# Residual tokens parked in DRAM during the first expert product; their SBUF as gate sums and gated one-hots

## The chip, the cores and the metric

The kernel runs on one core of one Trainium2 chip. Its engines are TensorE (PE, matmuls; PEld are its weight loads), VectorE (DVE), ScalarE (ACT), GpSimd (POOL) and SyncE (SP, which issues nearly all DMAs). Every engine works through its own queue in order. On-chip memory is SBUF (128 partitions) and PSUM (eight banks, where PE writes). The metric is the device time of one execution in microseconds, the median of the runs.

## The reference

256 tokens of width 1024 go through two layers (retention, then differential attention, each followed by an expert block) and a second network (two gated feed-forwards around a mixer); all of it in float32. The part that the change touches is the expert block `peer_ffn`, which stands in both layers. Cut to what matters:

```python
q   = (xc @ w_q).reshape(tokens, 8, 2, 128)            # 8 heads, 2 halves
sc  = einsum('thpd,hpnd->thpn', q, subkeys)            # 128 scores for each half
s1, i1 = top_k(sc[:, :, 0], 16); s2, i2 = top_k(sc[:, :, 1], 16)
cand = s1[..., :, None] + s2[..., None, :]             # 256 candidates per head
top, pos = top_k(cand, 16)                             # 16 experts per head, of 128 x 128
gate = softmax(top)
act  = gelu(einsum('ted,td->te', u[idx], xc))
out  = einsum('te,ted->td', gate * act, v[idx])
x = layer_norm(alpha * x + out)
```

## The kernel before

The kernel gathers nothing. It computes the gelu of *all* 16384 experts for all tokens as a dense product, multiplies by a dense gate that is zero for experts not chosen, and makes a second dense product with `v`. Line numbers are those of the profile.

**Weights.** `stream` (L130) loads weights as tiles `raw` of 512 KB, four buffers, issued by SyncE; `split` (L121) makes from each a rounded copy `wh` on ACT (L125) and the residue `wl` on DVE (L126), three buffers each, so that three matmuls give nearly float32 precision. The splits are planned with a priority 300 places ahead of their position.

**The first expert product.** `peer` (L1165) holds H, 128 partitions x 128 x 256 float32, as its largest tile: partition and the second index `i2` name the expert, the last index the token. Before the loop, `x_transposed` makes the transposed tokens `xT` from the residual tokens `xs` (two tiles of 128 x 1024 float32; the layer norm's scale and shift are put in on the way, and `xs` itself gets them only later, in `affine`). A loop over 16 units computes the queries and the scores; `route_keys` and `route` pick the experts, in the part of H that the product hasn't reached yet. Then the loop over `i2` = 0 to 127 runs: `gemm_a` (L142) makes 24 matmuls (L147 to L149) into one of two PSUM banks `mm`, and ACT writes the gelu to `H[:, i2]` (L1245).

**The gates.** From `i2` = `K0` = 44 on the gates are built in the same loop, four tokens to a group, 64 groups. `onehots` (L1430) makes on DVE the raw one-hots `o12` (L1442, row and column of each of a token's 128 slots; named `o` in the trace) and the column's one-hots times the gate values, `og` (L1443). `gates` (L1446) has PE multiply them (L1453) into a PSUM tile `gat`; ACT copies one half (L1457) and DVE adds the other (L1460) to the dense gate of four tokens, `gate`, 128 x 512 float32. One step later `apply` multiplies the rows of H that are there by the gate (DVE, L1461) and writes the gate into the rows to come (ACT, L1463). For those later rows the product's gelu can't simply overwrite H: for the `nt` tokens whose gate is already in H, ACT writes the gelu to a tile `gelu` (L1250) and DVE multiplies it in (L1251); the rest goes straight to H (L1248). How many groups there are per step is set by

```python
e = (i2 + 2 - K0) * (T // 4) // (NKEYS - KEND - K0)
```

The pool `peer_u` has one buffer of each of its tiles (`xT`, `iota`, `og`, `gate`, `gelu`), the pool `peer_oh` two of `o12`.

**The second expert product.** The pools of the first product are closed; four PSUM banks `acc` replace those of the gates. For every `i2`, ACT and DVE split `H[:, i2]` into `gh` (L1285) and `gl` (L1286), and twelve matmuls (L1276) add to the four banks. At `i2` = 8 `affine` (L331) loads the norm's scale and shift by two broadcast DMAs (`ln_g`, `ln_b`, L293) and applies them to `xs` on DVE (L338, L339). `normalise` at the end is the next reader of `xs`.

**What sets the order.** The program is written in the order above, and a planner orders each engine's queue when it is built: it takes what is ready by its own estimate of times, earlier instructions first, and gives a tile from a pool only when a buffer of it is free. Waits between engines are derived from who reads and writes what, by regions of a tile.

Of the kernel before, what the change touches and what calls it, by code (L numbers as in the profile page):

```python
# [10 lines left out]
F32 = mybir.dt.float32  # L11
F32R = mybir.dt.float32r
F16 = mybir.dt.float16
# [7 lines left out]
T = 256  # L21
D = 1024
# [8 lines left out]
NKEYS = 128  # L31
# [16 lines left out]

AHEAD = 300
K0 = 44  # L50
KEND = 2
FOXN = 2
GSTEP = 6
PACE = 1
# [13 lines left out]
class Ker:  # L68
    def __init__(s, tc, A, ctx):
        s.tc = tc  # L70
        s.nc = nc = tc.nc
        s.A = A
        s.ctx = ctx
        s.cst = ctx.enter_context(tc.tile_pool(name="cst", bufs=1))
        s.rawp = ctx.enter_context(tc.tile_pool(name="rawp", bufs=4))
        s.hlp = ctx.enter_context(tc.tile_pool(name="hlp", bufs=3))
        s.ident = s.cst.tile([128, 128], F32, name="ident")
        s.ahead = AHEAD
        s.hold = []
        s.psn = 0  # L80
        s.ssq = s.cst.tile([128, 2, 2], F32, name="ssq")
        small = s.cst.tile([128, NSMALL], F32, name="small")
        s.last_tr = [None, None]
        s.zeros = s.cst.tile([128, 256], BF16, name="zeros")
        nc.gpsimd.memset(s.zeros, 0.0)
        s.small = small
        at = 0
        for n, w in SMALL:
            setattr(s, n, small[:, at:at + w])
            at += w  # L90
        s.events = []
# [563 lines left out]
    def mixer(s, xs, units_r, units_f, units_g, units_ra, units_fb, units_o):  # L655
        nc, A = s.nc, s.A
        with ExitStack() as cx:
# [41 lines left out]
            with ExitStack() as c1:  # L699
# [61 lines left out]
                for i in range(8):  # L761
                    next(fox, None)
                    with s.after(s.mark):
                        if i + FOXN < 8:
                            e = i + FOXN
                            unit_r(1 + e // 4, e % 4, w["rv"[e // 4]])
                    if i == BDAT:
                        next(prep)
                        s.rwkv_blocks(0, 0, w, bd0)
                    if i >= 8 - NGATE:  # L770
                        with s.after(s.mark):
                            next(gates, None)
# [4 lines left out]
            with ExitStack() as c1:  # L777
# [9 lines left out]
                while nxt < 8 or live:  # L787
                    if nxt < 8 and len(live) < LIVE:
                        live.append((nxt, todo[nxt]))
                        nxt += 1  # L790
                    for it in list(live):
                        step += 1
                        if step >= GS0 and (step - GS0) % GSTEP == 0:
                            assert s.mark
                            with s.tc.issue_after(s.mark), s.tc.high_priority(offset=LOW):
                                next(gates, None)
                        for _ in range(2):
                            if next(it[1], None) is None:
                                if it in live:
                                    live.remove(it)  # L800
                                    if it[0] < 8 and it[0] % 2:
                                        live.append((8 + it[0] // 2, tails[it[0] // 2]))
                                break
# [361 lines left out]
    def peer(s, l, xs, units_q, units_u, units_v, ln):  # L1165
        nc, A = s.nc, s.A
        with ExitStack() as cx:
# [3 lines left out]
            H = hp.tile([128, NKEYS, T], F32, name="H")  # L1171
            cu = ExitStack()
            p = s.pool("peer_u", 1, cu)
            s.iota = p.tile([128, 128], F16, name="iota")
            nc.sync.dma_start(s.iota, A["iota"])
            with ExitStack() as ct:
                xT = s.x_transposed(p, xs, "xT", s.ln_cols(ln), s.pool("peer_t", 2, ct))
            po = s.pool("peer_oh", 2, cu)

            off = [K0 * T]  # L1180

            def carve(shape, dt=F32):
                n = int(np.prod(shape[1:]))
                words = n if dt != F16 else (n + 1) // 2
                ap = H.rearrange("p a b -> p (a b)")[:, off[0]:off[0] + words]
                off[0] += words
                assert off[0] <= NKEYS * T
                if dt != F32:
                    ap = ap.bitcast(dt)
                if len(shape) == 2:  # L1190
                    return ap
                names = "abcde"[:len(shape) - 1]
                return ap.rearrange("p (%s) -> p %s" % (" ".join(names), " ".join(names)),
                                    **{k: v for k, v in zip(names, shape[1:])})
# [7 lines left out]
            def restart():  # L1202
# [7 lines left out]
            rt = {"s16": carve([128, 2, 16, TOPK]), "i16": carve([128, 2, 16, TOPK], U32),  # L1210
                  "tmp": [carve([128, NKEYS]) for _ in range(4)]}
            def scores(c):
                ps = s.aux()[:, :T].rearrange("p (a b) -> p a b", a=2)
                for tt in range(2):
                    nc.tensor.matmul(ps[:, tt], qT[:, c, tt * 128:tt * 128 + 128], sk[:, c], start=True, stop=True)
                nc.scalar.activation(sc[:, :, c], ps, AF.Copy)
# [17 lines left out]
            g = 0  # L1234
            pend = []
            for i2 in range(NKEYS):
                ps = s.mm()[:, :T]
                s.gemm_a(next(units_u), xT, ps)
                if i2 < 2:
                    if i2 == 0:  # L1240
                        scores(15)
                    s.route_keys(rt, sc, 14 + i2)
                nt = 4 * g
                if nt == 0:
                    nc.scalar.activation(H[:, i2], ps, AF.Gelu_apprx_tanh)  # L1245
                else:
                    if nt < T:
                        nc.scalar.activation(H[:, i2, nt:], ps[:, nt:], AF.Gelu_apprx_tanh)  # L1248
                    ge = p.tile([128, T], F32, name="gelu")
                    nc.scalar.activation(ge[:, :nt], ps[:, :nt], AF.Gelu_apprx_tanh)  # L1250
                    nc.vector.tensor_tensor(H[:, i2, :nt], H[:, i2, :nt], ge[:, :nt], op=ALU.mult)  # L1251
                if 2 <= i2 < K0:
                    for _ in range(ROUTE_STEPS):
                        next(route, None)
                    if i2 == K0 - 1:
                        for _ in route:
                            pass
                elif i2 >= K0:
                    for f in pend:
                        f(i2 + 1)  # L1260
                        g += 1
                    e = (i2 + 2 - K0) * (T // 4) // (NKEYS - KEND - K0)
                    pend = [s.gates(H, p, s.onehots(p, po, rt, j), j) for j in range(g, min(e, T // 4))]
            assert g * 4 == T
            cu.close()
            cg.close()
            s.banks(cx, "acc", 4)
            p2 = s.pool("peer_v2", 3, cx)
            p = s.pool("peer_v", 1, cx)
# [11 lines left out]
            for i2 in range(NKEYS):  # L1281
# [3 lines left out]
                a = nc.scalar.activation(wh, H[:, i2], AF.Copy).ins  # L1285
# [11 lines left out]
            a, b, c = last  # L1297
# [129 lines left out]
                                         [128, 128, 2, 2]), AF.Copy)  # L1427
            yield

    def onehots(s, p, p2, rt, g):  # L1430

        nc = s.nc
        sh = [128, 8, 64, 2]
        t4 = slice(4 * g, 4 * g + 4)
        tok = lambda t: t[:, t4].rearrange("p t a e -> p (t a) e")[:, :, None, :].to_broadcast(sh)
        v = lambda t: t.rearrange("p t a (k e) -> p (t a) k e", e=2)
        o = p2.tile([128, 4, 2, 128], F16, name="o12")
        og = p.tile([128, 4, 2, 128], F16, name="og")  # L1440
        io = s.iota.rearrange("p (k e) -> p k e", e=2)[:, None].to_broadcast(sh)
        nc.vector.tensor_tensor(v(o), io, tok(rt["I"]), op=ALU.is_equal)  # L1442
        nc.vector.tensor_tensor(v(og), o[:, :, 1:2].to_broadcast([128, 4, 2, 128]), tok(rt["G"]), op=ALU.mult)  # L1443
        return o[:, :, 0], og

    def gates(s, H, p, oh2, g):  # L1446


        nc = s.nc
        o1, og = oh2  # L1450
        ps = s.pgat.tile([128, 4, 2, 128], F32, name="gat")
        for t in range(4):
            nc.tensor.matmul(ps[:, t], o1[:, t], og[:, t], start=True, stop=True)  # L1453
        pv = ps.rearrange("p t a i -> p a i t")
        ts = slice(4 * g, 4 * g + 4)
        gt = p.tile([128, NKEYS, 4], F32, name="gate")
        nc.scalar.activation(gt, pv[:, 1], AF.Copy, scale=1.0 / GSCALE)  # L1457

        def apply(k):
            nc.vector.scalar_tensor_tensor(gt, pv[:, 0], 1.0 / GSCALE, gt, op0=ALU.mult, op1=ALU.add)  # L1460
            nc.vector.tensor_tensor(H[:, :k, ts], H[:, :k, ts], gt[:, :k], op=ALU.mult)  # L1461
            if k < NKEYS:
                nc.scalar.activation(H[:, k:, ts], gt[:, k:], AF.Copy)  # L1463

        return apply
# [190 lines left out]
```

## Time and profile before

| | |
|---|---|
| median of 3 runs | 2747.91 us (2747.08 to 2750.75) |
| the profiled execution's own time | 2750.62 us |
| its span | 2748.8 us |
| PE busy | 2674.3 us, 97% |
| DVE busy | 2004.6 us, 73% |
| ACT busy | 1472.8 us, 54% |
| POOL busy | 7.8 us |
| DMA | 450.49 MB, mean 164 GB/s |

Matmuls are pipelined: a matmul of 256 columns is listed with 0.28 us, but the next begins 0.12 us later. Idle time of an engine is put down to the instruction before which it stood, with the instruction that released it. Where a wait is listed for PE, the matmul before it counts as busy until its modelled end.

### The profile page before, as it was taken

What the parts mean: (1) busy time and instruction counts of PE and PEld (TensorE: products, weight loads), DVE (VectorE), ACT (ScalarE), POOL (GpSimd) and SP (SyncE); (2) the same over time, 40 slices, a digit from 0 to 9 for tenths busy, and PEclk for the clock granted to TensorE, in tenths of its full rate; (3) what the DMA queues carried; (4) which work ended last, traced back from release to release, by engine and by line L of the source; (5) the groups of instructions that cost most, each with busy time, mean ns of one, the idle gap of its engine ahead of it and who ended that gap; (6) DMA issues with size and microseconds to landing.
All of it is one profiled execution on the core that took longest, in us unless ns stands there. A gap on an engine that the chain in (4) does not pass through costs nothing. (4 is left out here: it accounts for less than half of the span.)

```text
span 2748.8 us, 44032 instructions
## 1 busy us (share of the span) xinstructions
PE 2674.3 (97%) x16550; PEld 2360.8 (86%) x16550; DVE 2004.6 (73%) x3688; ACT 1472.8 (54%) x2575; POOL 7.8 (0%) x24
## 2 busy tenths in 40 slices
PE   9999999999999999999999999999999999999999
PEld 7789999988788888789999888888878887887887
DVE  7559968899666668789788997666687567665674
ACT  4445556555555555555466555555555465543554
POOL 0000000000000000000000000000000000000000
PEclk9999999999999999999999999999999999999999
DMA  6454554444566654345554445666655553222554
GB/s 209 154 183 164 185 178 161 154 146 154 191 193 194 195 193 162 99 161 181 178 165 152 152 154 181 194 192 193 196 173 187 190 168 109 70 70 67 171 187 151
DMA packets 124420, 450.49 MB, mean 164 GB/s; under 512 B 14336, under 2 KB 15120, under 8 KB 123952
## 3 DMA queue, kind: packets, MB, share of 16 engines
q1 hardware_dynamic: 124064, 447.62, 50.1%
q8 instruction: 130, 2.13, 0.3%
q14 instruction: 82, 0.67, 0.1%
q10 hardware_dynamic: 144, 0.07, 0.0%
HBM read 446.57 MB, written 1.05 MB: 163 GB/s over the span
## 5 line engine op out<-in xcount | busy, mean ns | idle before, releaser
L126 DVE TENSOR_TENSOR wl<-raw,wh 128x1024 fp32r<-128x1024 f32 x830 | 1014.6, 1223 | 430.6 <-ACT wh L125 429.3
L125 ACT ACTIVATE wh<-raw 128x1024 fp32r<-128x1024 f32 x830 | 879.3, 1060 | 671.3 <-PE mm L148 332.4
L147 PE MATMUL mm<-xT,wh 128*128 128x256 f32 x2384 | 685.9, 288 | 29.8 <-ACT gelu L1250 26.6
L149 PE MATMUL mm<-xT,wl 128*128 128x256 f32 x2384 | 677.3, 284 | 1.8 <-DVE wl L126 1.8
L148 PE MATMUL mm<-xT,wh 128*128 128x256 f32 x2384 | 677.7, 284 | 0.0
L147 PEld LDWEIGHTS mm<-xT,wh 128*128 128x128 f32 x2384 | 457.3, 192 | 39.7 <-ACT gelu L1250 33.4
L149 PEld LDWEIGHTS mm<-xT,wl 128*128 128x128 f32 x2384 | 457.7, 192 | 2.9 <-DVE wl L126 2.4
L148 PEld LDWEIGHTS mm<-xT,wh 128*128 128x128 f32 x2384 | 458.2, 192 | 0.8 <-DVE xT L261 0.3
L1276 PE MATMUL acc<-wl,gh 128*128 128x512 f32 x1024 | 318.4, 390 | 0.3
L1276 PE MATMUL acc<-wh,gl 128*128 128x512 f32 x1024 | 317.3, 390 | 0.0
L1276 PE MATMUL acc<-wh,gh 128*128 128x512 f32 x1024 | 279.2, 391 | 6.8 <-ACT gh L1285 6.8
L1285 ACT ACTIVATE gh<-H 128x256 fp32r<-128x256 f32 x256 | 106.5, 418 | 300.9 <-PE acc L1276 300.9
L1276 PEld LDWEIGHTS acc<-wh,gh 128*128 128x128 f32 x1024 | 192.8, 188 | 47.3 <-ACT gh L1285 7.2
L1276 PEld LDWEIGHTS acc<-wl,gh 128*128 128x128 f32 x1024 | 193.0, 188 | 41.4 <-DVE wl L126 1.1
L1276 PEld LDWEIGHTS acc<-wh,gl 128*128 128x128 f32 x1024 | 192.8, 188 | 40.0
L1286 DVE TENSOR_TENSOR gl<-H,gh 128x256 fp32r<-128x256 f32 x256 | 108.4, 425 | 121.9 <-PE acc L1276 121.9
L159 PE MATMUL mm<-xT,wh 128*128 128x512 f32 x406 | 145.9, 397 | 0.8 <-ACT wh L125 0.6
L160 PE MATMUL mm<-xT,wl 128*128 128x256 f32 x406 | 114.1, 281 | 0.8 <-DVE wl L126 0.8
L1443 DVE TENSOR_TENSOR og<-o,slotG 128x1024 f16<-128x1024 f16 x128 | 88.1, 688 | 29.8 <-PE gat L1453 28.8
L159 PE MATMUL aux<-xT,wh 128*128 128x512 f32 x294 | 105.0, 394 | 0.0
L182 PE MATMUL acc<-wl,xT 128*128 128x512 f32 x256 | 103.2, 404 | 0.0
L183 PE MATMUL acc<-wh,xT 128*128 128x512 f32 x256 | 101.8, 400 | 0.0
(539 smaller groups left out, 3859.7 us busy)
## 6 DMA issues: line engine op xcount, KB each, us to landing
raw<-peer_u SPq DMA_DIRECT2D x256, 512.0 KB, 3.8
raw<-peer_v SPq DMA_DIRECT2D x256, 512.0 KB, 4.6
raw<-ffn_w SPq DMA_DIRECT2D x132, 512.0 KB, 4.4
raw<-peer_q SPq DMA_DIRECT2D x32, 512.0 KB, 3.9
raw<-ret_qk SPq DMA_DIRECT2D x16, 512.0 KB, 3.4
raw<-ret_v SPq DMA_DIRECT2D x16, 512.0 KB, 4.0
raw<-ret_g SPq DMA_DIRECT2D x16, 512.0 KB, 3.8
raw<-ret_o SPq DMA_DIRECT2D x16, 512.0 KB, 3.2
```

The source lines that it names most:

```text
L125: a = nc.scalar.activation(h, ap, AF.Copy)
L126: d = nc.vector.tensor_tensor(l, ap, h.bitcast(F32), op=ALU.subtract)
L147: nc.tensor.matmul(out, w[0][:, c], x[0][:, d], start=start and d == 0, stop=False)
L148: nc.tensor.matmul(out, w[0][:, c], x[1][:, d], start=False, stop=False)
L149: nc.tensor.matmul(out, w[1][:, c], x[0][:, d], start=False, stop=stop and d == ND - 1)
L159: nc.tensor.matmul(ps, w[0][:, c], x, start=d == 0, stop=False)
L160: nc.tensor.matmul(ps[:, :T], w[1][:, c], both[:, d, 0], start=False, stop=False)
L182: nc.tensor.matmul(outs[tt], x[0][:, d, t], w[1][:, c], start=False, stop=False)
L183: mm = nc.tensor.matmul(outs[tt], x[1][:, d, t], w[0][:, c], start=False, stop=stop and j == 1)
L1276: mm = nc.tensor.matmul(accs[cb][tt], a[:, t], b[:, cb * 512:cb * 512 + 512], start=i2 == 0 and wi == 0, stop=i2 == NKEYS - 1 and wi == 2)
L1285: a = nc.scalar.activation(wh, H[:, i2], AF.Copy).ins
L1286: d = nc.vector.tensor_tensor(wl, H[:, i2], wh.bitcast(F32), op=ALU.subtract).ins
```

## The change

Three things. A DRAM tile `spill` is made for the two residual tiles. After `xT` is there, both tiles of `xs` are copied to it by GpSimd's DMA, and the memory of `xs` is used for other things until the first product is over: `xs[0]` as two gate sums (`gsum`, in place of the tile `gate`) and `xs[1]` as two tiles of gated one-hots (`gated`, in place of `og`), taken by the group's number modulo two. After the loop the residual tokens are copied back. Second, `gelu` moves to the pool `peer_oh`, which gets three buffers: three of `o12` and three of `gelu`. Third, `KEND` goes from 2 to 3, so that the last group of gates is built one step of `i2` earlier.

```diff
--- before.py
+++ after.py
@@ -48,7 +48,7 @@
 
 AHEAD = 300
 K0 = 44
-KEND = 2
+KEND = 3
 FOXN = 2
 GSTEP = 6
 PACE = 1
@@ -81,6 +81,8 @@
         s.ssq = s.cst.tile([128, 2, 2], F32, name="ssq")
         small = s.cst.tile([128, NSMALL], F32, name="small")
         s.last_tr = [None, None]
+        dram = ctx.enter_context(tc.tile_pool(name="dram", bufs=1, space=bass.MemoryType.DRAM))
+        s.spill = dram.tile([2, 128, D], F32, name="spill")
         s.zeros = s.cst.tile([128, 256], BF16, name="zeros")
         nc.gpsimd.memset(s.zeros, 0.0)
         s.small = small
@@ -1175,7 +1177,12 @@
             nc.sync.dma_start(s.iota, A["iota"])
             with ExitStack() as ct:
                 xT = s.x_transposed(p, xs, "xT", s.ln_cols(ln), s.pool("peer_t", 2, ct))
-            po = s.pool("peer_oh", 2, cu)
+            po = s.pool("peer_oh", 3, cu)
+
+            for tt in range(2):
+                nc.gpsimd.dma_start(s.spill[tt], xs[tt])
+            s.gsum = xs[0].rearrange("p (b i t) -> p b i t", b=2, t=4)
+            s.gated = xs[1].bitcast(F16).rearrange("p (b t a k) -> p b t a k", b=2, t=4, a=2)
 
             off = [K0 * T]
 
@@ -1246,7 +1253,7 @@
                 else:
                     if nt < T:
                         nc.scalar.activation(H[:, i2, nt:], ps[:, nt:], AF.Gelu_apprx_tanh)
-                    ge = p.tile([128, T], F32, name="gelu")
+                    ge = po.tile([128, T], F32, name="gelu")
                     nc.scalar.activation(ge[:, :nt], ps[:, :nt], AF.Gelu_apprx_tanh)
                     nc.vector.tensor_tensor(H[:, i2, :nt], H[:, i2, :nt], ge[:, :nt], op=ALU.mult)
                 if 2 <= i2 < K0:
@@ -1260,10 +1267,12 @@
                         f(i2 + 1)
                         g += 1
                     e = (i2 + 2 - K0) * (T // 4) // (NKEYS - KEND - K0)
-                    pend = [s.gates(H, p, s.onehots(p, po, rt, j), j) for j in range(g, min(e, T // 4))]
+                    pend = [s.gates(H, s.onehots(po, rt, j), j) for j in range(g, min(e, T // 4))]
             assert g * 4 == T
             cu.close()
             cg.close()
+            for tt in range(2):
+                nc.gpsimd.dma_start(xs[tt], s.spill[tt])
             s.banks(cx, "acc", 4)
             p2 = s.pool("peer_v2", 3, cx)
             p = s.pool("peer_v", 1, cx)
@@ -1427,7 +1436,7 @@
                                          [128, 128, 2, 2]), AF.Copy)
             yield
 
-    def onehots(s, p, p2, rt, g):
+    def onehots(s, p, rt, g):
 
 
 
@@ -1436,14 +1445,14 @@
         t4 = slice(4 * g, 4 * g + 4)
         tok = lambda t: t[:, t4].rearrange("p t a e -> p (t a) e")[:, :, None, :].to_broadcast(sh)
         v = lambda t: t.rearrange("p t a (k e) -> p (t a) k e", e=2)
-        o = p2.tile([128, 4, 2, 128], F16, name="o12")
-        og = p.tile([128, 4, 2, 128], F16, name="og")
+        o = p.tile([128, 4, 2, 128], F16, name="o12")
+        og = s.gated[:, g % 2]
         io = s.iota.rearrange("p (k e) -> p k e", e=2)[:, None].to_broadcast(sh)
         nc.vector.tensor_tensor(v(o), io, tok(rt["I"]), op=ALU.is_equal)
         nc.vector.tensor_tensor(v(og), o[:, :, 1:2].to_broadcast([128, 4, 2, 128]), tok(rt["G"]), op=ALU.mult)
         return o[:, :, 0], og
 
-    def gates(s, H, p, oh2, g):
+    def gates(s, H, oh2, g):
 
 
         nc = s.nc
@@ -1453,7 +1462,7 @@
             nc.tensor.matmul(ps[:, t], o1[:, t], og[:, t], start=True, stop=True)
         pv = ps.rearrange("p t a i -> p a i t")
         ts = slice(4 * g, 4 * g + 4)
-        gt = p.tile([128, NKEYS, 4], F32, name="gate")
+        gt = s.gsum[:, g % 2]
         nc.scalar.activation(gt, pv[:, 1], AF.Copy, scale=1.0 / GSCALE)
 
         def apply(k):
```

## Rows read from the trace of the kernel before

**Rows 1.** The page's engine table: busy us, share of the span, instructions.

```profile
PE 2674.3 (97%) x16550; PEld 2360.8 (86%) x16550; DVE 2004.6 (73%) x3688; ACT 1472.8 (54%) x2575; POOL 7.8 (0%) x24
```

**Rows 2.** Stretch, length; busy us of PE, PEld, DVE, ACT, POOL; granted clock; DMA share; GB/s.

```profile
400.00:500.00 100.00, 97.28 (x812) 94.92 (x812) 84.26 (x139) 61.81 (x131) 0.00 (x0) 1.00 0.50 163
500.00:600.00 100.00, 94.42 (x787) 91.64 (x786) 90.30 (x147) 57.51 (x131) 0.00 (x0) 1.00 0.46 150
600.00:687.00 87.00, 80.40 (x664) 77.13 (x663) 80.67 (x124) 48.63 (x113) 0.00 (x0) 1.00 0.46 151
687.00:691.00 4.00, 0.72 (x7) 0.51 (x5) 3.12 (x6) 1.77 (x5) 0.00 (x0) 1.00 0.43 137
692.00:695.00 3.00, 3.00 (x9) 2.32 (x8) 0.23 (x1) 0.42 (x1) 0.00 (x0) 0.52 0.95 355
...
1500.00:1600.00 100.00, 92.73 (x767) 89.37 (x768) 91.72 (x147) 56.84 (x131) 0.00 (x0) 1.00 0.46 149
```

**Rows 3.** Waits of PE, whole span: who for whom, us, times, longest.

```profile
PE mm L147 <- ACT gelu L1250: 26.6, 24, 1.4
PE acc L1276 <- ACT gh L1285: 6.8, 2, 3.4
...
PE gat L1453 <- DVE og L1443: 3.1, 4, 0.8
```

**Rows 4.** Timeline of waits at L147: start, us, engine, line, tiles, idle before.

```profile
436.85 0.61 PE L1453 MATMUL gat<-og,o 128*128 128x256 f16 x4
438.37 0.38 PE L147 MATMUL mm<-xT,wh 128*128 128x256 f32 x1 [0.91 <-ACT gelu L1250]
...
541.86 0.28 DVE L1251 TENSOR_TENSOR H<-H,gelu 128x124 f32<-128x124 f32 x1
...
542.00 0.61 PE L1453 MATMUL gat<-og,o 128*128 128x256 f16 x4
542.08 1.06 ACT L125 ACTIVATE wh<-raw 128x1024 fp32r<-128x1024 f32 x1 [1.42 <-PE mm L148]
...
543.20 0.59 ACT L1457 ACTIVATE gate<-gat 128x512 f32<-128x512 f32 x1
...
543.68 0.28 ACT L1250 ACTIVATE gelu<-mm 128x128 f32<-128x128 f32 x1
...
544.01 0.39 PE L147 MATMUL mm<-xT,wh 128*128 128x256 f32 x1 [1.40 <-ACT gelu L1250]
...
550.31 0.61 PE L1453 MATMUL gat<-og,o 128*128 128x256 f16 x4
...
550.67 0.36 PE L147 MATMUL mm<-xT,wh 128*128 128x256 f32 x1
```

**Rows 5.** Waits of DVE before L1443, and L1443 in the list of instructions.

```profile
DVE og L1443 <- PE gat L1453: 28.8, 62, 0.9
...
L1443 DVE TENSOR_TENSOR og<-o,slotG 128x1024 f16<-128x1024 f16 x128 | 88.1, 688 | 29.8 <-PE gat L1453 28.8
```

**Rows 6.** Timeline of the change from the first product to the second.

```profile
687.71 0.68 DVE L1461 TENSOR_TENSOR H<-H,gate 128x504 f32<-128x504 f32 x1
...
690.38 0.38 ACT L1250 ACTIVATE gelu<-mm 128x256 f32<-128x256 f32 x1 [1.59 <-DVE H L1251]
690.66 1.02 ACT L1285 ACTIVATE gh<-H 128x256 fp32r<-128x256 f32 x3
...
691.13 0.74 PE L1276 MATMUL acc<-wh,gh 128*128 128x512 f32 x2 [3.41 <-ACT gh L1285]
```

**Rows 7.** Where `xs` is first written, and the nearest DMA, with us to landing.

```profile
709.80 2.35 DVE L338 TENSOR_TENSOR x<-x,ln_g 128x1024 f32<-128x1024 f32 x2
...
ln_b<-ln SPq DMA_DIRECT2D x4, 512.0 KB, 5.8
```

## The prediction

> **What bounds the kernel now.** I read the page's engine table first: TensorE (PE) is busy for 97% of the span and VectorE (DVE) is the next engine [rows 1]. So only time in which PE stands still can be won, and the question is how much of it belongs to the stage that the change touches. That stage is the second part of each first expert product: the loop over `i2` in `peer`, from `K0` on, in which the gates are built beside the product. It lies at about 410 to 687 us in the first layer and 1380 to 1660 us in the second.
>
> The busy table by stretches [rows 2] shows what changes inside it. PE idles 2.7 us in 400 to 500, 5.6 us in 500 to 600 and 6.6 us in 600 to 687, while DVE's busy time goes from 84.3 of 100 to 90.3 of 100 to 80.7 of 87: the gated part of H grows, and with it DVE's multiplications. The second layer has the same shape (PE 92.7 of 100 in 1500 to 1600). Two more things stand there: from 687 to 691 PE is busy for 0.72 us of 4, and from 692 to 695 its granted clock is 0.52 of full speed, which is the lower of its two levels (1.2 against 2.4 GHz); before that fall it had stood still.
>
> PE's table of waits [rows 3] names the causes: 26.6 us in 24 waits for L1250, the partial gelu, 12 of them in each layer; 6.8 us in 2 waits for L1285 where the second product starts; 3.1 us in 4 waits for L1443, the gated one-hots. The timeline of one wait [rows 4] shows the chain. The row of L1251 at 541.86 reads the only `gelu` tile until 542.14. Before that ScalarE (ACT) may not write the next gelu; at 542.08 it takes up the next weight copy instead, then a gate copy, and writes that gelu from 543.68 on. The gelu is what empties a PSUM bank of the product, there are two, so PE's next step begins at 544.01. From the gate product at 542.00 that is 2.01 us. In the undisturbed case in the same rows (550.31 to 550.67) it is 0.36 us. So the wait costs 1.65 us where the table shows 1.40; the short kind (436.85 to 438.37) costs 1.16 where it shows 0.91. Each wait costs 0.25 us more than it shows.
>
> **The change part by part.**
>
> *Three gelu tiles in place of one.* The 24 waits cost 26.6 + 24 x 0.25 = 32.6 us. With three tiles a gelu waits for a multiplication three steps back, and the link at 542.14 is gone.
>
> *Two gate sums and two gated one-hots, in the memory of `xs`, and three raw one-hots.* The four waits for L1443 cost 3.1 + 4 x 0.25 = 4.1 us. DVE itself idles 28.8 us before L1443, waiting for PE to have read the only `og` [rows 5]; a second buffer lets DVE do one pair of one-hots more ahead (a pair is two operations of about 0.69 us, so 1.4 us). The gate sum's wait on ACT is off PE's path except where a gelu stands behind it, which is in the 24 already.
>
> What is late next is DVE. By stretches, one layer loses 2.7 + 3 x 0.25 = 3.5 us, 5.6 + 4 x 0.25 = 6.6 us and 6.6 + 7 x 0.25 = 8.4 us, 18.5 us in all. In the first two DVE idles 15.7 and 9.7 us, more than PE has to win. In the last it idles 6.3 us: it can't do the same work in 8.4 us less. With the pair done ahead, 7.7 us at the most; no engine is filled to the end, so I take 6.5. From the first two I take off 1 us, for a wait or two that find another cause. That is 3.5 + 6.6 - 1 + 6.5 = 15.6 us per layer.
>
> *The last gates one step earlier (`KEND` 3).* The number of groups is the same (64 per layer) and so is the work, spread over 81 steps in place of 82. What moves is the end: now the last multiplication of H by a gate (L1461) begins at 687.71, when the product's matmuls are through, and lasts 0.68 us; after that ACT still waits 1.59 us for the gelu tile (gelu at 690.38), copies gh at 690.66, and PE starts at 691.13 [rows 6]. With the change the last gate is a step earlier and no gelu waits for its tile. What is left of the 3.41 us is a weight copy that may already be running on ACT (1.06 us), a gelu (690.38 to 690.66) and gh up to PE's start (0.47 us), 1.6 us if they overlap a little with the product's end. I take a gain of 1.8 us; the ends are 0, if gh stays behind something else, and 3.4.
>
> *The clock.* The fall in 692 to 695 costs at least 0.48 x 3 = 1.4 us per layer. Waits of up to 1.40 us leave the clock at 1.00 in the stretches before; the wait of 3.41 us is followed by a fall. With 1.6 us I count half: 0.7 us.
>
> *The spill and the restore.* Two DMAs of 512 KB out and two back per layer, issued by GpSimd. No GpSimd DMA is in this trace; the nearest row is that of `ln_b`, 512 KB in 5.8 us on SyncE's queue. The spill has no reader or writer behind it until the first gated one-hot, over 100 us later. The restore may start when the last gate sum is read and must be in before L338, which writes `xs` at 709.80 [rows 7]: 709.80 - 687.71 - 0.68 = 21.4 us for work of 2 x 5.8 = 11.6 us if the two don't overlap at all. Hidden, then: price 0 to 11.6 us per layer, and no gain, since transfers are only added. It shares the DMA engines with the second product's weights and with `ln_g` and `ln_b`, which load at the same place; the share is already 0.95 in 692 to 695. I put 0.5 us per layer for a late weight tile. If the cover is gone, DVE stands at L338 and the weight residues behind it (L126) are late for PE. The new wait before the first write into `xs` (for the spill) costs nothing for the same 100 us.
>
> *The order.* The instruction order is a planner's, made when the program is built, so every queue of the stage will be ordered anew. What that does elsewhere I take as 0, between -2 and +2 us, which is what the single small waits of PE are worth (the 1.59 us wait in rows 6 is the size of one).
>
> Sum per layer: 15.6 + 1.8 + 0.7 - 0.5 = 17.6 us, twice 35 us. The profiled execution took 2750.62 us (span 2748.8), so it would take 2715.6; the median of the runs is 2747.91, 2.7 us lower, so I predict 2713 us.
>
> **The rivals.**
>
> *Everything comes back.* All of 18.5 + 3.4 + 1.4 = 23.3 us per layer, 46.6 in all: 2701 us. For it: the three causes are all lack of a buffer. Against it: DVE's 6.3 us in the last stretch. Chance 0.15.
>
> *DVE fills up earlier.* Its work that now waits moves in front of PE's needs, and the last stretch gives nothing. Then the first two stretches give about half, 5 us, and the transition 1.8: 2 x 6.8 = 14 us, 2734 us. For it: DVE 93% busy in 600 to 687. Against: L126 is planned ahead of everything else on DVE. Chance 0.16.
>
> *It doesn't do what it says.* The gelu stays behind a gate copy on ACT because that waits for DVE anyway (in rows 4 the gate copy at 543.20 stands directly ahead of the late gelu), and the waits only get another name: 2748 us, within 4. Chance 0.06.
>
> *Slower: the restore is late.* The place is L338 on DVE at 709.80. DVE now spends 2.35 us there on the first two operations and PE doesn't stop, so some 3 us of lateness are free; from there each us costs PE one, in both layers. It decides the sign when it eats 17.6 us, so when the restore lands 20.6 us after 709.80, 42 us after the last gate, 3.6 times as long as the 11.6 us above. At 25 us late it is 2 x (22 - 17.6) = 9 us slower: 2757 us. For it: a GpSimd DMA isn't priced in this trace and DVE is nearly full as it starts. Against: the margin. Chance 0.05.
> The Trainium skill ("SBUF — State Buffer", section "SBUF: two separate sides") says that GpSimd can't write the descriptors of its DMAs while DVE runs an operation in a mode that takes both of its ports, which would speak for this rival. Its section "Who interferes with whom" adds that `tensor_tensor` has no such mode, and DVE's rows between 687 and 709 us here are all tensor-tensor forms; no run so far shows a GpSimd DMA beside them.
>
> **How the numbers follow.** The forecast has 0.58, with a range of its own from 2704 to 2724 (gains of 44 to 24 us: the last stretch and the transition at their ends). The 80% range goes from 2699 to 2736: it takes in the full return and DVE filling up, and leaves out no change and the late restore. About 0.2% of this time, 5.5 us, is what a measurement can tell from no change. Faster by more: 0.15 + 0.58 + 0.16, less 0.01 for the tails, 0.88. Within: 0.06. Slower: 0.05 and 0.01 for an order that turned out badly, 0.06.
>
> **What would show it.** PE's waits for L1250 fall from 24 to a few, those for L1443 vanish; DVE's wait before L1443 shrinks and DVE is busy for over 95% towards the end of the stage; the wait for L1285 is about 1.6 us; the stretch after it shows the clock at 1.00 in at least one layer; the restore has landed well before L338 and L338 doesn't wait. Wrong would be: as many waits before L147 with another releaser (L126 or a gate copy), a stage as long as before, DVE standing at L338, or a gain outside these two stages.

## The result, and the profile after

The changed kernel takes 2720.55 us (median of 4 runs, 2718.90 to 2721.53) against 2747.49 us before (4 runs): 26.9 us less, a ratio of 0.990 with a 95% interval from 0.9883 to 0.9917. A second set of runs of the same kernel gave 2720.81 us and 0.989 (0.9871 to 0.9910). The forecast was 35 us less, 2713 us, in a range from 2699 to 2736. The profiled execution took 2719.57 us (span 2717.8), 31.0 us less than the profiled one of before.

Lines have moved by two to nine: L147 is now L149, L1250 L1257, L1251 L1258, L1276 L1285, L1285 L1294, and L338 is L340; the gate sum and the gated one-hots show as `x`, since they lie in the memory of `xs` (L1443 is L1452, L1457 L1466, L1461 L1470, L1463 L1472).

PE's waits, whole span, against [rows 3]:

```profile
PE mm L149 <- ACT gelu L1257: 8.4, 6, 1.4
PE acc L1285 <- ACT gh L1294: 3.4, 2, 1.7
```

Of 24 waits for the gelu 6 are left, all of the long kind, three in each layer; the waits for the one-hots are gone; the wait at the second product's start has halved (3.41 us in [rows 6], 1.71 now). Where the six stand is in the busy table of the first layer, against [rows 2] (columns as there; the product ends at about 673 us now):

```profile
400.00:500.00 100.00, 100.00 (x842) 98.30 (x841) 88.02 (x149) 61.87 (x138) 0.00 (x0) 1.00 0.52 167
500.00:600.00 100.00, 100.00 (x842) 98.33 (x842) 94.45 (x154) 59.96 (x140) 0.00 (x0) 1.00 0.51 165
600.00:666.00 66.00, 61.78 (x515) 59.80 (x514) 62.46 (x97) 36.13 (x86) 0.00 (x0) 1.00 0.47 155
...
672.00:676.00 4.00, 2.29 (x15) 1.93 (x14) 3.19 (x6) 2.35 (x6) 0.54 (x1) 1.00 0.92 267
676.00:680.00 4.00, 4.00 (x19) 3.13 (x18) 2.72 (x7) 1.52 (x3) 0.00 (x0) 1.00 0.93 304
```

PE doesn't stop at all between 400 and 600 us. Every wait for the gelu that is left in this layer lies after 600 us, where DVE is busy for 62.46 of 66 us. Behind the start of the second product (676 to 680) the clock is at 1.00, where it had fallen to 0.52 before.

The copies: the timeline of the first layer's end (start, us, engine, line, what) and the issues with KB and us to landing.

```profile
670.70 0.54 POOL L1275 DMA_DIRECT2D x<-spill  x1 [457.12 <-DVE H L1258]
...
674.92 0.54 POOL L1275 DMA_DIRECT2D x<-spill  x1 [3.67 <-ACT gh L1294]
674.98 0.73 PE L1285 MATMUL acc<-wh,gh 128*128 128x512 f32 x2 [1.71 <-ACT gh L1294]
...
692.15 2.35 DVE L340 TENSOR_TENSOR x<-x,ln_g 128x1024 f32<-128x1024 f32 x2
```

```profile
spill<-x POOLq DMA_DIRECT2D x4, 512.0 KB, 3.5
...
x<-spill POOLq DMA_DIRECT2D x4, 512.0 KB, 6.5
```

The second restore is issued at 674.92; the longest landing of any of these copies is 8.8 us, so `xs` is whole by about 684, 8 us ahead of L340 (L338 in [rows 7]), which doesn't wait.

### The profile page after: what moved, and what is told of

Its sections match the earlier page's. It is cut to its first block, busy times and chain, and to the rows that moved or that the text cites. A ratio compares the mean times of both kernels' runs of the same rounds, so it can differ in the third digit from the quotient of the medians.

```text
span 2717.8 us, 44068 instructions
## 1 busy us (share of the span) xinstructions
PE 2666.7 (98%) x16550; PEld 2359.1 (87%) x16550; DVE 1998.3 (74%) x3688; ACT 1462.2 (54%) x2573; POOL 12.2 (0%) x32
## 5 line engine op out<-in xcount | busy, mean ns | idle before, releaser
L149 PE MATMUL mm<-xT,wh 128*128 128x256 f32 x2384 | 687.5, 289 | 11.6 <-ACT gelu L1257 8.4
L150 PE MATMUL mm<-xT,wh 128*128 128x256 f32 x2384 | 679.8, 285 | 0.0
L149 PEld LDWEIGHTS mm<-xT,wh 128*128 128x128 f32 x2384 | 458.6, 193 | 17.1 <-ACT gelu L1257 10.1
L150 PEld LDWEIGHTS mm<-xT,wh 128*128 128x128 f32 x2384 | 459.3, 193 | 0.8 <-DVE xT L263 0.3
L1285 PE MATMUL acc<-wl,gh 128*128 128x512 f32 x1024 | 317.7, 390 | 0.3
L1285 PE MATMUL acc<-wh,gl 128*128 128x512 f32 x1024 | 317.1, 390 | 0.0
L1285 PE MATMUL acc<-wh,gh 128*128 128x512 f32 x1024 | 278.3, 390 | 3.4 <-ACT gh L1294 3.4
L1294 ACT ACTIVATE gh<-H 128x256 fp32r<-128x256 f32 x256 | 106.5, 418 | 298.5 <-PE acc L1285 298.5
L1285 PEld LDWEIGHTS acc<-wh,gh 128*128 128x128 f32 x1024 | 192.2, 188 | 43.6 <-ACT gh L1294 3.8
L1285 PEld LDWEIGHTS acc<-wl,gh 128*128 128x128 f32 x1024 | 192.3, 188 | 40.8 <-DVE wl L128 1.1
L1285 PEld LDWEIGHTS acc<-wh,gl 128*128 128x128 f32 x1024 | 192.2, 188 | 40.2 <-DVE gl L1295 0.5
L1452 DVE TENSOR_TENSOR x<-o,slotG 128x1024 f16<-128x1024 f16 x128 | 88.3, 690 | 20.5 <-PE gat L1462 18.6
```

The costliest lines, as they stand in the source:

```text
L149: nc.tensor.matmul(out, w[0][:, c], x[0][:, d], start=start and d == 0, stop=False)
L150: nc.tensor.matmul(out, w[0][:, c], x[1][:, d], start=False, stop=False)
L1285: mm = nc.tensor.matmul(accs[cb][tt], a[:, t], b[:, cb * 512:cb * 512 + 512], start=i2 == 0 and wi == 0, stop=i2 == NKEYS - 1 and wi == 2)
```

## Experiments

Two numbers are used below. One is the median of the runs. The other, an estimate, is what the trace's clock record leaves of a profiled span when the clock's falls are taken out: PE does about half as much at 0.50 of full speed (19 matmuls of the second product in 4 us at 1.00 above, 11 in 4 us at 0.57 in kend2 below), so half of the time at 0.50 is counted as lost. Before, 31.2 us stood at 0.50, so 15.6 were lost and 2748.8 - 15.6 = 2733.2 remain; after, 29.2 and 2703.2 (again: 39.3 and 2701.1). The times of one kernel scatter by up to 14 us (one_gsum, 2731.1 to 2745.6 us, at mean granted clocks from 0.999 to 0.993); the remainder, called "at full clock" below, shows the schedule better. It comes from one profile for each run and isn't exact either: the two profiles of the changed kernel differ by 2.1 us, and in every run the last 4 to 6 us at 0.50 come after PE's last matmul, where nothing is lost by them. Differences of 2 or 3 us say nothing.

Each ratio is to the kernel before as measured beside that run (medians from 2746.7 to 2750.5 us).

| run | edit | median, us | ratio to before (95%) | waits for gelu, us and times | wait at the second product, us | span without the clock's loss |
|---|---|---|---|---|---|---|
| before | | 2747.5 | | 26.6, 24 | 6.8 | 2733.2 |
| after | | 2720.6 | 0.990 (0.9883 to 0.9917) | 8.4, 6 | 3.4 | 2703.2 |
| after_again | after, unchanged | 2720.8 | 0.989 (0.9871 to 0.9910) | 8.5, 6 | 3.4 | 2701.1 |
| two_gelu | before, two gelu tiles | 2754.4 | 1.0017 (1.0008 to 1.0025) | 28.8, 26 | 7.2 | 2735.4 |
| only_kend | before, KEND 3 | 2743.9 | 0.9983 (0.9974 to 0.9992) | 27.7, 28 | 3.2 | 2727.6 |
| one_gelu | after, one gelu tile | 2735.0 | 0.9955 (0.9941 to 0.9969) | 17.8, 20 | 3.2 | 2718.4 |
| one_gsum | after, one gate sum | 2738.3 | 0.9957 (0.9940 to 0.9974) | 21.1, 16 | 3.4 | 2722.6 |
| one_gated | after, one og | 2731.9 | 0.9932 (0.9919 to 0.9945) | 10.6, 10 | 3.4 | 2707.3 |
| kend2 | after, KEND 2 | 2733.8 | 0.9945 (0.9931 to 0.9958) | 8.4, 6 | 7.2 | 2709.1 |
| copies2 | after, every copy twice | 2721.5 | 0.9896 (0.9881 to 0.9911) | 8.4, 6 | 3.4 | 2703.2 |
| gelu5 | after, five gelu, two o12 | 2716.5 | 0.9880 (0.9865 to 0.9895) | 1.8, 2 | 8.2 | 2702.5 |
| early_gates | after, uneven gate rate | 2717.7 | 0.9888 (0.9873 to 0.9903) | 8.8, 6 | 3.2 | 2706.7 |
| gelu5_k4 | gelu5, KEND 4 | 2718.0 | 0.9884 (0.9869 to 0.9899) | 1.8, 2 | 5.9 | 2699.4 |
| gelu5_early | gelu5, uneven gate rate | 2719.8 | 0.9898 (0.9883 to 0.9913) | 2.0, 2 | 7.3 | 2701.0 |

**Which buffer was it?** Four runs, one buffer each.

```diff
 # two_gelu, in the kernel before
-                    ge = p.tile([128, T], F32, name="gelu")
+                    ge = po.tile([128, T], F32, name="gelu")
```

> The kernel before with one thing changed: two gelu tiles in place of one; one og, one gate sum, KEND 2 and no copies, as before. Theory A (the gelu tile alone holds PE up; what the second og and gate sum give is DVE and ACT time that PE doesn't need): most of the 32.6 us of waits for L1250 go, 2722 to 2728 us. Theory B (the three shortages are one: DVE, stopped 28.8 us at its only og, is late with the gelu multiplication too, so that a second gelu tile is used up as well): half the waits stay, 2731 to 2740 us.

```diff
 # one_gelu, in the changed kernel
-                    ge = po.tile([128, T], F32, name="gelu")
+                    ge = p.tile([128, T], F32, name="gelu")
```

> The changed kernel with one gelu tile in place of three; all else as changed (two og, two gate sums, three o12, KEND 3, copies). Theory A: the waits before the first product's matmuls come back nearly whole, 18 to 24 of them, and the transition's wait with its gelu; 2738 to 2747 us. Theory B: with og and gate sums doubled DVE is in time, and half of the gain stays: 2730 to 2737 us.

```diff
 # one_gated
-        og = s.gated[:, g % 2]
+        og = s.gated[:, 0]
```

> The changed kernel with one buffer of gated one-hots (index 0 for every group); all else as changed. Theory A: DVE idles some 28 us before L1452 again, but PE loses only in the last stretch, where DVE has no room: 2 to 6 us more, 2722 to 2727 us. Theory B: half of the waits for the gelu come back, 2730 us or more.

```diff
 # one_gsum
-        gt = s.gsum[:, g % 2]
+        gt = s.gsum[:, 0]
```

> The changed kernel with one gate sum (index 0 for every group); all else as changed. Theory A: ACT waits some 30 us for the multiplication by the gate again, ahead of a gelu in its queue in a few places: 0 to 5 us more, 2720 to 2726 us. Theory B: ACT's order is what delays the gelu, and half of the waits come back: 2730 us or more.

A second gelu tile alone gives nothing: 26 waits in place of 24, and a median above before's. Both theories missed that. ACT's waits, whole span, first those of the kernel before, then of two_gelu:

```profile
ACT gate L1457 <- DVE H L1461: 30.9, 41, 2.1
...
ACT H L1463 <- DVE gate L1460: 25.0, 22, 1.8
...
ACT gelu L1250 <- DVE H L1251: 16.0, 24, 1.6
```

```profile
ACT H L1463 <- DVE gate L1460: 32.1, 26, 1.8
ACT gate L1457 <- DVE H L1461: 31.4, 40, 2.1
...
ACT gelu L1250 <- DVE H L1251: 4.7, 8, 0.7
```

The gelu's own wait for its tile falls from 16.0 to 4.7 us, and ACT's waits at the only gate sum, for DVE to have used it (L1457) or added to it (L1463), grow from 55.9 to 63.5 us. But PE's waits don't stand directly behind these. One of them in two_gelu:

```profile
601.86 0.33 DVE L1251 TENSOR_TENSOR H<-H,gelu 128x176 f32<-128x176 f32 x1
...
602.02 1.06 ACT L125 ACTIVATE wh<-raw 128x1024 fp32r<-128x1024 f32 x1 [1.52 <-PE mm L148]
...
603.09 0.59 ACT L1457 ACTIVATE gate<-gat 128x512 f32<-128x512 f32 x1
...
603.57 0.33 ACT L1250 ACTIVATE gelu<-mm 128x184 f32<-128x184 f32 x1
...
603.94 0.39 PE L147 MATMUL mm<-xT,wh 128*128 128x256 f32 x1 [1.40 <-ACT gelu L1250]
```

ACT idles for 1.52 us until PE has finished a step of the product (L148, which reads the weight tile `wh` that the next copy writes). Then come the weight copy, a gate copy that waits for nothing, and only then the gelu for which PE stands. All 26 waits of two_gelu have such a weight copy in front, with ACT's idle time before it ended by L148, and so have 22 of the 24 of the kernel before (542.08 in [rows 4] is one); in the other two the chain begins with a wait of a gate copy for DVE. This makes the two kinds of wait in the kernel before: 1.40 us with a gate copy between the weight copy and the gelu, 0.91 without. The weight copy isn't urgent: there are three tiles `wh`, used in turn, so it is for a step that begins some 6 us after the one that stands (an estimate, from 2.9 us a step).

The tile is short all the same. This gelu needs the tile that is two gelus back, and its multiplication ends at 602.19, when ACT has already turned to the weight copy. In the first layer of two_gelu the tile came free between 0.4 us before and 0.6 us after the start of that copy in all 13 waits, and in the kernel before, with one tile, within 0.4 us of it in all 12. So DVE is late by one gelu where there is one tile and by two where there are two. With one gate sum in the changed kernel ACT's two waits are back, and with them 16 waits of PE:

```profile
ACT x L1466 <- DVE H L1470: 33.4, 48, 2.4
...
ACT H L1472 <- DVE x L1469: 20.5, 14, 1.8
```

There too a weight copy stands ahead of every late gelu, and in seven of the first layer's eight waits the tile, now three gelus back, came free within 0.4 us of that copy's start: with one gate sum, three tiles are used up as well. How one gate sum makes DVE late isn't shown. A rival stays untested: every run has its queues ordered anew by the planner, and none changed the order alone, with the gelu ahead of the weight copy and the buffers as they were.

At full clock, taking one buffer away from the changed kernel costs 19.4 us for the gate sum, 15.2 us for the gelu tiles and 4.1 us for og. With KEND (5.9 us, below) that is 44.6 us, where the whole change is worth 30.0: they overlap. Of the parts alone only two were run: the gelu tile gives nothing, KEND 5.6 us at full clock. Theory B's place held for one_gelu and one_gsum (one_gelu has theory A's number of waits, 20, in theory B's time); in two_gelu theory B's reason held for the tiles, more strongly than it was put, but its other half, the only og that makes DVE late, isn't shown: in the changed kernel one og costs 4.1 us. For og alone the cost at full clock is theory A's, though the median (11 us more, with a lower clock) lies in theory B's place.

**KEND.** One run with it alone, one without it (`KEND = 3` for 2 in the kernel before, `KEND = 2` for 3 in the changed one).

> The kernel before with KEND 3 in place of 2 and nothing else. Theory A: the start of the second product still waits for the one gelu tile, a step earlier in DVE's queue: its wait falls from 3.4 to about 2 us per layer and the waits in the first product stay: 2742 to 2748 us. Theory B (KEND is a large part of the change, as taking it away cost 13 us): 2738 us or less.

> The changed kernel with KEND 2 in place of 3; all else as changed. By the prediction's step, the last gate ends on the path again: the wait where the second product starts grows from 1.7 us to 2.5 to 3.4 us per layer, perhaps with a fall of the clock behind it; 2 to 6 us more, 2722 to 2727 us. Rival: that wait was the single gelu tile's alone, and KEND gives nothing: 2719 to 2722 us.

Alone it halves the wait at the second product's start (6.8 to 3.2 us in both layers together) and leaves the others (28 in place of 24, 27.7 us in place of 26.6); 4.3 us less than the 2748.2 us of before measured beside it, theory A. Without it that wait is 7.2 us, and a fall of the clock follows it in both layers. Here kend2, the wait and the stretch behind it:

```profile
674.00:678.00 4.00, 0.40 (x5) 0.11 (x2) 3.56 (x7) 2.36 (x6) 0.54 (x1) 1.00 0.77 182
678.00:682.00 4.00, 4.00 (x11) 3.13 (x12) 1.16 (x4) 0.97 (x3) 0.54 (x1) 0.57 1.00 366
```

The median rose by 13 us, twice the 6 us expected at most. At full clock it is 5.9 us, of which 3.8 are the wait; the rest of the 13 is the clock (45.2 us at 0.50 against 29.2), 3.4 us of the loss at the two transitions and the remainder at other places, which KEND doesn't touch.

**The copies.**

```diff
-            for tt in range(2):
+            for tt in (0, 1, 0, 1):
                 nc.gpsimd.dma_start(s.spill[tt], xs[tt])
...
-            for tt in range(2):
+            for tt in (0, 1, 0, 1):
                 nc.gpsimd.dma_start(xs[tt], s.spill[tt])
```

> The changed kernel with every copy of the residual tokens made twice (two spills and two restores of each tile, one behind the other). If the copies are hidden, as the prediction has it, but for 0.5 us per layer: 2720 to 2723 us, and L340 begins later only if the second restore isn't in by then. Rival: they take DMA time from the weights at the start of the second product, 2 to 4 us per layer: 2725 us or more.

Twice the copies cost nothing that can be measured: 2721.5 us, and 2703.2 at full clock, as with one set. But the cover is then used up: L340 waits 0.22 us for the DMA:

```profile
693.56 1.23 DVE L340 TENSOR_TENSOR x<-x,ln_g 128x1024 f32<-128x1024 f32 x1 [0.22 <-DMA x<-spill]
```

**What keeps the last six waits?** The timeline of one of them in the changed kernel:

```profile
641.96 0.69 DVE L1258 TENSOR_TENSOR H<-H,gelu 128x224 f32<-128x224 f32 x2
...
644.12 1.06 ACT L127 ACTIVATE wh<-raw 128x1024 fp32r<-128x1024 f32 x1 [2.06 <-PE mm L150]
...
645.14 0.59 ACT L1466 ACTIVATE x<-gat 128x512 f32<-128x512 f32 x1
...
645.62 0.62 ACT L1257 ACTIVATE gelu<-mm 128x232 f32<-128x232 f32 x2
...
646.04 0.39 PE L149 MATMUL mm<-xT,wh 128*128 128x256 f32 x1 [1.39 <-ACT gelu L1257]
```

DVE takes two multiplications by a gelu at once at 641.96: it was behind by as many gelus as there are tiles, until the first of the two ended at 642.34. But ACT idles up to 644.12, for PE (L150) and not for a tile, and only then, behind a weight copy and a gate copy, writes two gelus in a row. So the tiles had run out for a time, and the order of ACT's queue made the wait as long as it is; in the other two waits of this layer, too, the tile was free before the weight copy began (0.7 and 2.1 us). Two experiments give more tiles or less late work.

```diff
 # gelu5
-            po = s.pool("peer_oh", 3, cu)
+            po = s.pool("peer_oh", 2, cu)
+            pg = s.pool("peer_ge", 5, cu)
...
-                    ge = po.tile([128, T], F32, name="gelu")
+                    ge = pg.tile([128, T], F32, name="gelu")
```

> The changed kernel with five gelu tiles and two raw one-hots in place of three and three; all else as changed. Theory A (the three waits left per layer are a shortage of gelu tiles while DVE is behind): they go, 4 to 10 us less, 2711 to 2717 us. Theory B (DVE is full there, so PE loses the same time under another name): 2719 to 2723 us.

```diff
 # early_gates
-                    e = (i2 + 2 - K0) * (T // 4) // (NKEYS - KEND - K0)
+                    u = (i2 + 2 - K0) / (NKEYS - KEND - K0)
+                    e = int(T // 4 * (u + 0.25 * u * (1 - u)) + 1e-9)
```

> The changed kernel with the gates' groups spread unevenly over the steps: one per step at first, 0.6 per step at the end, in place of 0.79 throughout, so that DVE has more work where it idled (400 to 600 us) and less in the last stretch. Theory A (DVE's lack of room in the last stretch is what keeps three waits per layer): they go, 6 to 10 us less, 2711 to 2715 us. Theory B (the waits are the order that the planner found, whatever DVE's room): 2718 us or more.

With five tiles the waits do go (the last stretch of gelu5 first), but DVE's work is only pushed to the end, and PE waits for it there:

```profile
600.00:666.00 66.00, 65.91 (x552) 64.21 (x550) 61.90 (x95) 38.04 (x88) 0.00 (x0) 1.00 0.50 164
```

```profile
671.00:675.00 4.00, 0.17 (x1) 0.17 (x2) 3.96 (x8) 1.62 (x7) 0.68 (x2) 0.95 0.92 261
675.00:679.00 4.00, 4.00 (x12) 3.14 (x13) 1.34 (x4) 0.81 (x3) 0.41 (x1) 0.62 0.93 379
```

From 671 to 675 DVE is busy for 3.96 of 4 us and PE for 0.17; the wait is 4.1 us per layer in place of 1.7. At full clock that is 2702.5 against 2703.2 us, nothing: theory B by its reason, though the median, 4 us lower, lies in theory A's place (the intervals of the two ratios overlap). Gates done earlier leave 6 waits, two of the first layer's three now between 500 and 600 us. Theory A of that run fell.

```profile
500.00:600.00 100.00, 97.16 (x814) 94.84 (x813) 94.01 (x153) 59.38 (x138) 0.00 (x0) 1.00 0.49 159
```

Last, five tiles with the gates' end a step earlier (KEND 4), and five tiles with the uneven rate.

> Five gelu tiles and two raw one-hots, and KEND 4 in place of 3. With five tiles the three waits in the last stretch had gone, but the second product's start came later (a wait of 4.1 us in place of 1.7, with a fall of the clock behind it in both layers). Theory A (DVE's leftover work is only pushed to the end, and one more step without new gates clears it under the product): that wait is back at 1.7 us or less without the fall, 5 to 9 us less than with KEND 3, 2708 to 2712 us. Theory B (DVE is full, and gates that must be done a step earlier push it further behind): waits return before the first product's matmuls, 2715 to 2720 us.

> Five gelu tiles and two raw one-hots, KEND 3, and the gates' groups spread unevenly (one per step at first, 0.6 per step at the end). Theory A (DVE's backlog at the end is what is left, and work done early removes it): no wait in the first product but the transition's 1.7 us, 2706 to 2712 us. Theory B (the uneven rate only moves the waits, as it did with three tiles, to 500 to 600 us): 2714 us or more.

Both have 2 waits for the gelu in place of 6 and still 5.9 us (4.2 and 1.7) and 7.3 us at the second product's start. At full clock they are 3.8 and 2.2 us below the changed kernel's first profile, but 1.7 and 0.1 us below its second; their medians, 2718.0 and 2719.8, can't be told from its 2720.6. The times lie in theory B's place in both, but its reason, new waits before the first product's matmuls, didn't come about. No version was found that is surely better.

**The clock, once more.** The changed kernel again, unchanged.

> The changed kernel once more, for the clock alone: its profiled execution lost 14.6 us to the lower clock, all of it outside the two expert blocks' transitions, where the kernel before lost 3.4 of its 15.6 us. Theory A (the falls outside these places come at random, and the transitions' falls are really gone): times spread over several us with the granted clock, 2717 to 2724 us, none of the falls at the two transitions, and the loss elsewhere between 8 and 15 us. Theory B (the changed schedule draws more falls later on): the loss elsewhere is 14 us or more again, and all times are near 2721 us.

2720.81 us (2713.63 to 2722.53, with mean granted clocks from 0.998 to 0.993). Neither transition has a fall in either profile of this kernel. Elsewhere the loss was 19.7 us in this profile, 14.6 in the first, and 12.2 before, most of it in the second network, where the order of work is nearly the same (before and after, the last 4,000 instructions of PE differ at 22 places, the last 800 of DVE at 14 and the last 650 of ACT at none). So theory A's place held and its bound did not; whether the changed kernel really draws more falls there stays open.

## Why the prediction was nearly right

The sign, the places and the range were right; the gain was 27 us where 35 were forecast. Point by point:

- *The waits in the first product, 15.6 us per layer.* By the rule of the prediction (0.25 us on top of what a wait shows) one layer lost 18.5 us and now loses 4.2 + 3 x 0.25 = 5.0: 13.5 us came back. In the first two stretches all of the 10.1 us did, where 9.1 were counted; in the last 3.4 of 8.4, where 6.5 were counted. This is the mis-sized term. DVE's 6.3 us of idle time (7.7 with the pair ahead) were a bound that the prediction nearly exhausted; gelu5 speaks for the bound, since the time that is saved there comes back at the end. In the last stretch DVE came to 94.6% (62.46 of 66 us), just under the 95% named as a sign.
- *Its cause.* "With three tiles a gelu waits for a multiplication three steps back, and the link at 542.14 is gone" puts all 24 waits, 32.6 us, down to the tile. two_gelu moved that link one gelu back and gained nothing, since DVE fell back by one gelu more. The chain was read rightly (weight copy, gate copy, gelu), but it is the order of ACT's queue, and more tiles alone don't change it. The gate sum was given no price of its own ("off PE's path except where a gelu stands behind it, which is in the 24 already"); taking the second one away costs 19.4 us, the most of all parts. The rival "it doesn't do what it says" had the right time for the second gelu tile alone, but not the reason: in 22 of the 24 waits ACT stood for PE ahead of a weight copy, and a gate copy in the chain began without a wait. The sum was built from PE's losses by stretch and from DVE's room, not from a price for each buffer, so these errors didn't reach it. That the three doublings together did what was expected of the gelu tiles is in part luck.
- *The second product's start.* 1.8 us per layer forecast, 3.41 - 1.71 = 1.7 measured. KEND brings it: alone 1.8, with the one gelu tile, and without it nothing.
- *The clock.* 0.7 us per layer was counted, for one fall of two. Both are gone, which is worth 1.7 us each (3.4 us at half speed). But the profiled span lost 14.6 us to the clock after and 15.6 before: what the transitions gave back went to falls at places that the change doesn't touch. At full clock the gain is 30.0 us, against the forecast's 2 x (15.6 + 1.8 - 0.5) = 33.8. The profiled executions differ by 31.0 us and the medians by 26.9; where the other executions lost the difference isn't traced.
- *The copies.* 0.5 us per layer counted, nothing measured. The spill has over 100 us of cover, the restore 8 us. The late restore didn't come about; with each copy made twice it would just have begun. Restores land in 6.5 us at the median beside a DVE with tensor-tensor work and at a DMA share of 0.92, against 4.5 us for a weight tile of the same size; which of the two makes the 2 us isn't told apart. The Trainium skill's rule on DVE and the descriptors of GpSimd's DMAs ("SBUF — State Buffer", section "SBUF: two separate sides") isn't put to the test by this: between 670 and 692 us all of DVE's rows are tensor-tensor forms (one of them with a scalar), and no run has a restore beside another form.

## What to carry to other kernels

A wait is put down to the instruction that released it, but in an in-order queue that instruction may be late because of what stands ahead of it: look at what that is, and what it waited for, before pricing one buffer. Where several single buffers link the same engines, one more of one of them may give nothing (here the gelu tile) and all together nearly everything; price them as one step. And where the next engine is over 90% busy, take its idle time as an upper bound: here, in the last stretch, PE got back 3.4 us where DVE had idled 6.3.

## What the runs showed of the hardware

At the start of the second product (two layers, fourteen profiles), PE's waits of 1.6 and 1.7 us were never followed by a fall of the clock; waits of 3.4 us and more were, in all layers but one (two_gelu, first layer, 3.6 us). A fall lasted 3.4 us, now and then 6.8, at 0.50, so a wait of 3.4 us there costs about 5 (an estimate: half of 3.4 on top). The length of the wait alone doesn't decide it. In the second network the same wait of 1.79 us (before the same matmul, for DVE's weight residue) was followed by a fall at once in the changed kernel, at 2242.8, and not in the kernel before, at 2276.5; first the changed kernel, then the one before:

```profile
2243.00:2244.00 1.00, 1.00 (x8) 1.00 (x8) 1.00 (x2) 0.99 (x4) 0.00 (x0) 0.71 0.30 33
2244.00:2245.00 1.00, 1.00 (x6) 1.00 (x6) 1.00 (x2) 1.00 (x2) 0.00 (x0) 0.50 0.89 242
```

```profile
2277.00:2278.00 1.00, 1.00 (x11) 1.00 (x10) 1.00 (x2) 1.00 (x3) 0.00 (x0) 1.00 0.43 90
2278.00:2279.00 1.00, 1.00 (x10) 1.00 (x10) 1.00 (x2) 1.00 (x2) 0.00 (x0) 1.00 0.97 291
```
